# The last RMSNorm of a two-layer diffusion step: weight on ScalarE, factor on VectorE in larger pieces, and the last square in two halves

## The chip, the cores and the metric

The kernel runs on one core of one Trainium2 chip. The metric is the device time of one execution in microseconds (us); several executions are timed and the median is taken. A hardware profile of one further execution gives the trace that the text reads.

## The reference, cut to what matters

Two groups of 128 tokens (a context pass and a denoising step) go through two layers; the model width is 2048. Every layer is a mixer and a gated FFN, each behind an RMSNorm, and a last RMSNorm ends the step:

```
def rmsnorm(x, g):
    xf = x.astype(jnp.float32)
    y = xf * lax.rsqrt(jnp.mean(xf * xf, axis=-1, keepdims=True) + EPS)
    return (y * g.astype(jnp.float32)).astype(x.dtype)
...
        x = x + gt1 * m
        h = rmsnorm(x, g_norm_ffn[l]) * (1 + sc2) + sh2
        x = x + gt2 * conv_ffn(h, w_ffn_up[l], w_ffn_conv[l], b_ffn_conv[l], w_ffn_down[l])
    return rmsnorm(x, g_final), ab_ctx, c_ctx
```

The change concerns the last line, and the sum of squares of the three norms before it and of the last.

## The kernel before, in words

**Layout.** The residual stream `x` lies in SBUF with the features on the 128 partitions, as 16 chunks of 128 features by 256 tokens (128 of each group). A weight matrix comes from HBM in tiles of 1024 KB (SyncE's queue), and every fp32 weight tile is split into a high part `wh` (ScalarE, line 221) and a low part `wl` (VectorE, line 222), in halves of 128x1024, with four buffers of each. TensorE makes three matmuls per 128x128 block (lines 338, 339, 342: `wh` by the high activations, `wh` by the low ones, `wl` by the high ones). At the last chunks before a norm (`QUIET`) the halves are split in two steps of 128x512.

**A chunk's end.** `residual` (line 617) adds a finished chunk to `x` by two VectorE instructions, one for each group of tokens. Where a norm follows, `stat_add` squares the chunk on ScalarE (line 172) and GpSimd adds it to a running sum `sqacc` (line 176); the last chunk's square is not added but kept in `sq`. This is so in the down projections' second half of the inner features (`down`, with `q == NQ - 1`), and in the mixers' output projections.

**The norm.** `stat_rstd` has TensorE sum `sqacc` (line 201) and the last `sq` (line 202) over the partitions, for the one group and then for the other; VectorE scales the result (`rv`, line 184), GpSimd takes the power -1/2 (`rr`, line 188), VectorE makes a diagonal matrix for each group (`diag`, line 208), and TensorE spreads it over the partitions (line 216), so that the factor of every token stands in PSUM on all partitions (`rb`). For the norms inside the layers `modulate` then works out `hx`, chunk by chunk: `nt` (VectorE, line 558; one half scaled by VectorE, line 564, the other by ScalarE, line 567), the high part (ScalarE, line 568), and the low part (VectorE or GpSimd, line 553). `first_three` feeds TensorE with three products at once as the chunks appear (lines 324 to 326), shifted against each other by two chunks.

**The end of the program.** After the last norm's `spread`, 16 VectorE instructions (line 1153) multiply each chunk by the final weight (a value for each partition) and by `rb`; after every four of them a DMA of four chunks, 512 KB, goes to the output (line 1156).

**What sets the order.** Instructions are put in order for each engine when the program is built, by a scheduler that runs the program in a simulated timeline; where the code says so (`keep_in_program_order`, used in `modulate` and `first_three` before layer 1's FFN), the written order holds among the marked instructions. Unmarked ones, such as the splits of weights, are placed around them. So an edit can move instructions elsewhere in the program.

Of the kernel before, what the change touches and what calls it, by code (L numbers as in the profile page):

```python
# [13 lines left out]
AF = mybir.ActivationFunctionType  # L14
ALU = mybir.AluOpType
# [3 lines left out]
P = 128  # L19
D = 2048  # L20
KD = D // P
T = 128
NT = 2 * T
# [10 lines left out]
NQ = 2  # L34
# [51 lines left out]
def step_kernel(ctx: ExitStack, tc: tile.TileContext, A: dict):  # L86
    nc = tc.nc
    pe, dve, act, pool, sp = nc.tensor, nc.vector, nc.scalar, nc.gpsimd, nc.sync
# [20 lines left out]
    def T_(pl, shape, tag, dt=F32, bufs=None):  # L109
        kw = {} if bufs is None else {"bufs": bufs}  # L110
        return pl.tile(shape, dt, tag=tag, name=nm(tag), **kw)
# [8 lines left out]
    def C(name):  # L120
        a, w = _AT[name]
        return cst[:, a:a + w]
# [7 lines left out]
    x = T_(keep, [P, KD, NT], "x")  # L130
# [17 lines left out]
    def step():  # L148
        for g in list(chains):
            if next(g, chains) is chains:  # L150
                chains.remove(g)
# [12 lines left out]
    def stat_add(st, src, n):  # L164

        st["n"] += 1
        if st["n"] == 1:
            st["acc"] = T_(keep, [P, NT], "sqacc")
            act.activation(st["acc"], src, AF.Square)
            return  # L170
        sq = T_(tmp, [P, NT], "sq", bufs=2)
        act.activation(sq, src, AF.Square)  # L172
        if st["n"] == n:
            st["last"] = sq
        else:
            pool.tensor_tensor(out=st["acc"], in0=st["acc"], in1=sq, op=ALU.add)  # L176

    def rstd(cols, n, factor=1.0, out=None):
# [170 lines left out]
    stage = ["ab"]  # L349
# [83 lines left out]
    def feature_step():  # L433

        l, j, q = FEATS[feat["i"]]
        t, c = divmod(feat["t"], 2)
        if c == 0:
            feat["raw"] = T_(wpool, [P, 4, 512], "araw", bufs=2)
            sp.dma_start(out=feat["raw"], in_=A["w_ada"][l, j, q, t])
        feature_sum((l, j, q), t, c, feat["raw"],  # L440
                    T_(feat["pool"], [P, D], "junk").rearrange("p (g n) -> p g n", g=4))
        feat["t"] += 1
        if feat["t"] == 8:
            biased(l, j, q)
            feat["i"] += 1
            feat["t"] = 0
# [10 lines left out]
    def row_step(until=len(ROWS)):  # L457
        if later:
            later.pop(0)()
        if ada["i"] >= until:  # L460
            return
        l, j, q = ROWS[ada["i"]]
        if ada["i"] < 8:
            return pair_step(l, j, q)
        t, g = divmod(ada["t"], 4)
        on_dve = ada["i"] in SUMMED
        if g == 0:
            ada["raw"] = T_(wpool, [P, 4, 512], "araw", bufs=2)
            sp.dma_start(out=ada["raw"], in_=A["w_ada"][l, j, q, t])
        raw = ada["raw"]  # L470
        if on_dve:
            if g % 2:
                feature_sum((l, j, q), t, g // 2, raw, T_(ada["pool"], [P, 4, 512], "junk", BF16, bufs=1))
        elif pinned[0]:
            if g == 1 and t:
                sum_rows(t - 1, ada["last"])
            if g == 3:
                ada["last"] = raw
                if t == 3:
                    last = ada["last"]  # L480
                    later.append(lambda: None)
                    later.append(lambda: sum_rows(3, last))
        elif g == 3:
            sum_rows(t, raw)
        ada["t"] += 1
        if ada["t"] == 16:
            later.extend([lambda: biased(l, j, q)] if on_dve else ada_finish(l, j, q))
            ada["i"] += 1
            ada["t"] = 0
# [25 lines left out]
    def pump(rows, feats=0.0, until=None):  # L515

        until = until or RLIMIT[stage[0]]
        step()
        ada["due"] += rows
        while ada["due"] >= 0.25:  # L520
            if ada["i"] >= until and not later:
                ada["due"] = 0.0
                break
            dve_or_none = ada["i"] >= until or ada["i"] in SUMMED
            ada["due"] -= 0.25 if dve_or_none else 0.25 * ada["pew"]
            row_step(until)
        feat["due"] += feats
        while feat["due"] >= 1.0 and feat["i"] < FLIMIT[stage[0]]:
            feat["due"] -= 1.0
            feature_step()  # L530
# [83 lines left out]
    def residual(ps, l, which, c, st=None):  # L614
        for g in range(2):
            s = slice(g * T, (g + 1) * T)
            dve.scalar_tensor_tensor(out=x[:, c, s], in0=ps[:, s],  # L617
                                     scalar=mod[:, l, 3 * which + 2, c, g:g + 1],
                                     in1=x[:, c, s], op0=ALU.mult, op1=ALU.add)
        if st is not None:  # L620
            stat_add(st, x[:, c], KD)
# [429 lines left out]
    def ffn(hx, W, ready, todo, l, st):  # L1051
        xh, xl = (lambda k: hx[:, k, :NT]), (lambda k: hx[:, k, NT:2 * NT])
        product = lambda: ready.pop(0) if ready else gemm(W.chunk(), xh, xl, between=todo.pop(0) if todo else None)
        WD = Weights(A["w_down"][l], KQ, TB)
        cw = ada["cw"]
        with tc.tile_pool(name=f"ffn{l}", bufs=1) as fp, banks(f"pffn{l}") as pf:
            feat["pool"] = pf
            feat["due"] = 0.0
            T_(fp, [P, SHIFT // 4], "pad")

            def conv(m):
                early = l > 0 and bool(ready)
                pin = tc.keep_in_program_order if early else lambda i: i
                ps = product()
                y = T_(fp, [P, NT], "cv", bufs=3)
                pin(act.activation(y, ps, AF.Identity, scale=cw[:, 1, m:m + 1], bias=cw[:, 3, m:m + 1]))  # L1066
                y3 = y.rearrange("p (g t) -> p g t", g=2)
                p3 = ps.rearrange("p (g t) -> p g t", g=2)
                pin(dve.scalar_tensor_tensor(out=y3[:, :, 1:], in0=p3[:, :, :T - 1],  # L1069
                                             scalar=cw[:, 0, m:m + 1], in1=y3[:, :, 1:],  # L1070
                                             op0=ALU.mult, op1=ALU.add))
                pin(dve.scalar_tensor_tensor(out=y3[:, :, :T - 1], in0=p3[:, :, 1:],  # L1072
                                             scalar=cw[:, 2, m:m + 1], in1=y3[:, :, :T - 1],
                                             op0=ALU.mult, op1=ALU.add))
                if early:
                    W.ahead(pin)
                return y

            def up(q):
                gs = []  # L1080
                for i in range(q * KQ, (q + 1) * KQ):
                    rate = 0 if i < LATE else FRATE["up"]
                    fine[0] = False
                    gate = conv(i)
                    pump(0, rate)
                    val = conv(NFF + i)
                    pump(0, rate)
                    act.activation(gate, gate, AF.Silu)
                    dve.tensor_tensor(out=val, in0=gate, in1=val, op=ALU.mult)
                    g = T_(fp, [P, ROW], "g", F32R, bufs=KQ)  # L1090
                    split(g[:, :NT], g[:, NT:2 * NT], val)
                    gs.append(g)
                    if l == 0 and i == LATE - 1:
                        load_row()
                return gs

            def down(gs, q):
                for c in range(KD):
                    quiet = q == NQ - 1 and c >= KD - QUIET[0]
                    fine[0] = quiet  # L1100
                    ps = gemm(WD.chunk(), lambda k: gs[k][:, :NT], lambda k: gs[k][:, NT:2 * NT])
                    residual(ps, l, 1, c, st if q == NQ - 1 else None)
                    pump(0, 0 if quiet else FRATE["down"])

            for q in range(NQ):
                gs = up(q)
                if q == 0:
                    ensure(l, 5)
                down(gs, q)
            while feat["i"] < FLIMIT[stage[0]]:  # L1110
                feature_step()


    with banks("pab") as ppool["ada"]:
# [5 lines left out]
        for c in range(KD):  # L1120
            sq = T_(tmp, [P, NT], "sq", bufs=2)
# [27 lines left out]
    st = stat_init()  # L1149
    ffn(hx, W, ready, todo, 1, st)  # L1150
    rb = norm_scale(st)
    for c in range(KD):
        dve.scalar_tensor_tensor(out=x[:, c], in0=x[:, c], scalar=C("gfin")[:, c:c + 1], in1=rb,  # L1153
                                 op0=ALU.mult, op1=ALU.mult)
        if c % 4 == 3:
            sp.dma_start(out=A["o_y"][:, c - 3:c + 1], in_=x[:, c - 3:c + 1])

# [132 lines left out]
```

## Time and profile before

| what | value |
|---|---|
| time, three runs | 2353.25 us median (2352.32 to 2356.36) |
| the profiled execution's own time | 2353.05 us |
| its span in the trace | 2351.3 us, so 1.75 us lie around it |
| TensorE matmul | 2304.8 us busy, 98% of the span |
| VectorE, ScalarE, GpSimd | 1780.2, 1163.3, 144.8 us busy |
| the end of the span, from the last product on | about 15 us, without large matmuls |

A row of a timeline has the start and the length in us, then engine, line, operation, output <- inputs, shape, and in brackets how long the engine sat idle ahead of it and what released it. A row with x2 is two like instructions from the start of the first to the end of the last. A line's number is that of the kernel before; in the changed kernel the same statements stand two lines lower from line 178 on, and four lower at the end.

### The profile page before, as it was taken

How to read it: one execution, taken by the hardware profiler on the slowest of the kernel's cores; microseconds unless marked ns; L12 is line 12 of the kernel's file. 1: busy time of each engine (PE TensorE's matmuls, PEld its weight loads, DVE VectorE, ACT ScalarE, POOL GpSimd, SP SyncE). 2: the span in 40 equal slices, each digit the busy share in tenths (PEclk: the TensorE clock that was granted, in tenths of full speed). 3: DMA queues.
4: the chain of work that ended last, by engine and by line, in shares of the span. 5: the costliest groups of instructions: out<-in, count | busy, mean ns of one | idle time of the engine just before them, and what ended most of it. 6: DMA issues, size and time to landing. Idle time of an engine off the chain costs nothing. (4 is left out here: it accounts for less than half of the span.)

```text
span 2351.3 us, 47128 instructions
## 1 busy us (share of the span) xinstructions
PE 2304.8 (98%) x19654; PEld 2190.2 (93%) x19654; DVE 1780.2 (76%) x2662; ACT 1163.3 (49%) x1835; POOL 144.8 (6%) x133
## 2 busy tenths in 40 slices
PE   7999999999999999999999999999999999999997
PEld 6788878799999999999989999898999999999997
DVE  3667554579999999999968889887899755666654
ACT  4346553465554355554455555446555434555542
POOL 0002001100000000001220000022000000000011
PEclk9999999999999999999999999999999999999998
DMA  9887778777777877777767788786677555555553
GB/s 383 338 324 261 256 277 315 306 290 267 267 269 272 309 263 257 264 262 271 293 235 256 262 310 298 300 316 243 221 265 269 198 194 190 192 196 198 196 188 118
DMA packets 92421, 610.81 MB, mean 260 GB/s; under 512 B 9968, under 2 KB 17840, under 8 KB 20528
## 3 DMA queue, kind: packets, MB, share of 16 engines
q1 hardware_dynamic: 92208, 607.80, 70.2%
q8 instruction: 154, 2.52, 0.4%
q14 instruction: 59, 0.48, 0.1%
HBM read 603.01 MB, written 4.75 MB: 258 GB/s over the span
## 5 line engine op out<-in xcount | busy, mean ns | idle before, releaser
L221 ACT CAST wh<-raw 128x1024 fp32r<-128x1024 f32 (+1 forms) x788 | 793.4, 1013 | 947.5 <-PE acc L339 765.1
L222 DVE TENSOR_TENSOR wl<-raw,wh 128x1024 fp32r<-128x1024 f32 (+1 forms) x788 | 922.6, 1186 | 345.2 <-ACT wh L221 326.2
L338 PE MATMUL acc<-hx,wh 128*128 128x256 f32 x3808 | 1058.9, 279 | 5.6 <-ACT hx L568 4.6
L339 PE MATMUL acc<-hx,wh 128*128 128x256 f32 x3808 | 1056.4, 278 | 0.6 <-DVE hx L553 0.6
L342 PE MATMUL acc<-hx,wl 128*128 128x256 f32 x3808 | 1056.5, 278 | 0.0
L338 PEld LDWEIGHTS acc<-hx,wh 128*128 128x128 f32 x3808 | 715.8, 188 | 32.4 <-issue 10.9
L342 PEld LDWEIGHTS acc<-hx,wl 128*128 128x128 f32 x3808 | 716.1, 188 | 10.3 <-issue 9.2
L339 PEld LDWEIGHTS acc<-hx,wh 128*128 128x128 f32 x3808 | 716.8, 188 | 6.3 <-issue 5.0
L429 DVE CUSTOM_DVE_ANT_0 junk<-araw,condb 128x2048 f32<-128x2048 f32 (+1 forms) x176 | 404.0, 2295 | 0.0
L339 PE MATMUL acc<-g,wh 128*128 128x256 f32 x1408 | 388.3, 276 | 0.0
L342 PE MATMUL acc<-g,wl 128*128 128x256 f32 x1408 | 388.0, 276 | 0.0
L338 PE MATMUL acc<-g,wh 128*128 128x256 f32 x1408 | 387.8, 276 | 0.0
L339 PEld LDWEIGHTS acc<-g,wh 128*128 128x128 f32 x1408 | 264.3, 188 | 0.0
L342 PEld LDWEIGHTS acc<-g,wl 128*128 128x128 f32 x1408 | 264.1, 188 | 0.0
L338 PEld LDWEIGHTS acc<-g,wh 128*128 128x128 f32 x1408 | 264.0, 188 | 0.0
L176 POOL TENSOR_TENSOR sqacc<-sqacc,sq 128x256 f32<-128x256 f32 x62 | 83.4, 1344 | 1579.5 <-issue 1291.6
L1066 ACT ACTIVATE cv<-acc,convw 128x256 f32<-128x256 f32 x176 | 98.4, 559 | 3.6 <-PE acc L342 2.0
L617 DVE SCALAR_TENSOR_TENSOR x<-acc,mod,x 128x128 f32<-128x128 f32 x192 | 58.1, 344 | 54.7 <-PE acc L342 54.1
L1069 DVE SCALAR_TENSOR_TENSOR cv<-acc,convw,cv 128x254 f32<-128x254 f32 x176 | 83.8, 476 | 4.6 <-ACT cv L1066 4.6
L1072 DVE SCALAR_TENSOR_TENSOR cv<-acc,convw,cv 128x254 f32<-128x254 f32 x176 | 84.4, 480 | 3.7
L452 PE MATMUL ada<-araw,condw 128*32 128x512 f32 x576 | 79.3, 616 | 4.5 <-DMA araw<-w_ada 4.5
L303 PE MATMUL acc<-wh,hx 128*128 128x256 f32 x256 | 70.3, 281 | 0.9 <-ACT dv L977 0.9
(238 smaller groups left out, 2125.6 us busy)
## 6 DMA issues: line engine op xcount, KB each, us to landing
araw<-w_ada SPq DMA_DIRECT2D x178, 1024.0 KB, 5.5
raw<-w_up SPq DMA_DIRECT2D x176, 1024.0 KB, 4.8
raw<-w_down SPq DMA_DIRECT2D x88, 1024.0 KB, 4.8
raw<-w_in_c SPq DMA_DIRECT2D x48, 1024.0 KB, 6.0
raw<-w_in_ab SPq DMA_DIRECT2D x19, 1024.0 KB, 7.2
raw<-w_out_ab SPq DMA_DIRECT2D x16, 1024.0 KB, 6.9
raw<-w_out_c SPq DMA_DIRECT2D x16, 1024.0 KB, 6.1
condb<-w_ada SPq DMA_DIRECT2D x12, 1024.0 KB, 7.1
```

The lines of the kernel that those rows point to most:

```text
L176: pool.tensor_tensor(out=st["acc"], in0=st["acc"], in1=sq, op=ALU.add)
L221: pin(act.copy(out_hi, src))
L222: pin(dve.tensor_tensor(out=out_lo, in0=src, in1=out_hi.bitcast(F32), op=ALU.subtract))
L303: pe.matmul(ps, hi, wh[:, s], start=a, stop=False)
L338: fixed(pe.matmul(ps[:, :n], wh, xh(k), start=(i == 0), stop=False))
L339: fixed(pe.matmul(ps[:, :n], wh, xl(k), start=False, stop=False))
L342: fixed(pe.matmul(ps[:, :n], wl, xh(k), start=False, stop=(i == last)))
L429: tc.keep_in_program_order(dve.tensor_tensor_reduce(out=junk, in0=raw, in1=condb[:, c].rearrange("p (g n) -> p g n", g=4), scale=1.0, scal ...
L452: i = pe.matmul(ada["ps"][32 * g:32 * g + 32, :], condw[:, 4 * t + g, :], raw[:, g], start=(t == 0), stop=(t == 3), skip_group_check=True)
L1066: pin(act.activation(y, ps, AF.Identity, scale=cw[:, 1, m:m + 1], bias=cw[:, 3, m:m + 1]))
L1069: pin(dve.scalar_tensor_tensor(out=y3[:, :, 1:], in0=p3[:, :, :T - 1], scalar=cw[:, 0, m:m + 1], in1=y3[:, :, 1:], op0=ALU.mult, op1=ALU.add))
L1072: pin(dve.scalar_tensor_tensor(out=y3[:, :, :T - 1], in0=p3[:, :, 1:], scalar=cw[:, 2, m:m + 1], in1=y3[:, :, :T - 1], op0=ALU.mult, op1=A ...
```

## The change

It has three parts. The final weight is applied by ScalarE inside the last `down`, in place, behind each chunk's square. After the last norm only the factor `rb` is left to apply, by five VectorE `tensor_tensor` instructions over 2, 4, 4, 4 and 2 chunks, each with a DMA of its own to the output. And the last chunk's square is made as two halves (one for each group of tokens) at the norms behind stage "ab": before layer 1's mixer, before layer 1's FFN, and the last.

```
         sq = T_(tmp, [P, NT], "sq", bufs=2)
-        act.activation(sq, src, AF.Square)
         if st["n"] == n:
+            for s in ([slice(0, NT)] if stage[0] == "ab" else [slice(0, T), slice(T, NT)]):
+                act.activation(sq[:, s], src[:, s], AF.Square)
             st["last"] = sq
         else:
+            act.activation(sq, src, AF.Square)
             pool.tensor_tensor(out=st["acc"], in0=st["acc"], in1=sq, op=ALU.add)
...
                     residual(ps, l, 1, c, st if q == NQ - 1 else None)
+                    if l == 1 and q == NQ - 1:
+                        act.activation(x[:, c], x[:, c], AF.Identity, scale=C("gfin")[:, c:c + 1])
                     pump(0, 0 if quiet else FRATE["down"])
...
     rb = norm_scale(st)
-    for c in range(KD):
-        dve.scalar_tensor_tensor(out=x[:, c], in0=x[:, c], scalar=C("gfin")[:, c:c + 1], in1=rb,
-                                 op0=ALU.mult, op1=ALU.mult)
-        if c % 4 == 3:
-            sp.dma_start(out=A["o_y"][:, c - 3:c + 1], in_=x[:, c - 3:c + 1])
+    for c, n in ((0, 2), (2, 4), (6, 4), (10, 4), (14, 2)):
+        dve.tensor_tensor(out=x[:, c:c + n], in0=x[:, c:c + n], op=ALU.mult,
+                          in1=rb[:, None, :].to_broadcast([P, n, NT]))
+        sp.dma_start(out=A["o_y"][:, c:c + n], in_=x[:, c:c + n])
```

TensorE's and GpSimd's rows stand in the same order in both programs. Three places show how rows move on the others.

ScalarE at the end of the program, from chunk 14's weights on, before (`wh` is a weight's high part, `sq` a square):

```order
L221 CAST wh_27566<-raw_27564 128x512 x2
L221 CAST wh_27572<-raw_27564 128x512 x2
L172 ACTIVATE sq_27561<-x_76 128x256
L221 CAST wh_27652<-raw_27650 128x512 x2
L221 CAST wh_27658<-raw_27650 128x512 x2
L172 ACTIVATE sq_27647<-x_76 128x256
L172 ACTIVATE sq_27733<-x_76 128x256
```

and of the change, with a row that scales `x` in place (line 1106) behind each square:

```order
L223 CAST wh_27582<-raw_27580 128x512 x2
L223 CAST wh_27588<-raw_27580 128x512 x2
L177 ACTIVATE sq_27576<-x_76 128x256
L223 CAST wh_27669<-raw_27667 128x512 x2
L1106 ACTIVATE x_76<-x_76,cst_74 128x256
L223 CAST wh_27675<-raw_27667 128x512 x2
L177 ACTIVATE sq_27663<-x_76 128x256
L1106 ACTIVATE x_76<-x_76,cst_74 128x256
L174 ACTIVATE sq_27750<-x_76 128x128 x2
L1106 ACTIVATE x_76<-x_76,cst_74 128x256
```

A scaling row comes behind each of the 16 squares, once with two casts between, and the last square is two rows.

VectorE from the last residual to the end, before (`misc` is the factor in PSUM):

```order
L617 SCALAR_TENSOR_TENSOR x_76<-acc_27664,mod_77,x_76 128x128 x2
L184 TENSOR_SCALAR rv_27742<-misc_27737 128x2
L208 TENSOR_SCALAR diag_27746<-cst_74,rr_27744 128x128 x2
L1153 SCALAR_TENSOR_TENSOR x_76<-x_76,cst_74,misc_27749 128x256 x16
L1279 UNCONDITIONAL_BRANCH
```

and of the change:

```order
L619 SCALAR_TENSOR_TENSOR x_76<-acc_27681,mod_77,x_76 128x128 x2
L186 TENSOR_SCALAR rv_27761<-misc_27756 128x2
L210 TENSOR_SCALAR diag_27765<-cst_74,rr_27763 128x128 x2
L1157 TENSOR_TENSOR x_76<-x_76,misc_27768 128x512
L1157 TENSOR_TENSOR x_76<-x_76,misc_27768 128x1024 x3
L1157 TENSOR_TENSOR x_76<-x_76,misc_27768 128x512
```

Sixteen rows have become five; each of the five is followed by its DMA on SyncE's queue.

ScalarE before layer 1's FFN, where `modulate` makes chunks 10 to 14 (`nt`, then the high part in `hx`) while weights are split for `first_three`; before:

```order
L221 CAST wh_19260<-raw_19158 128x1024
L567 ACTIVATE nt_19119<-nt_19119,mod_77,scl_78 128x128
L568 CAST hx_19032<-nt_19119 128x256
L567 ACTIVATE nt_19125<-nt_19125,mod_77,scl_78 128x128
L221 CAST wh_19279<-raw_19160 128x1024
L568 CAST hx_19032<-nt_19125 128x256
L567 ACTIVATE nt_19131<-nt_19131,mod_77,scl_78 128x128
L568 CAST hx_19032<-nt_19131 128x256
L567 ACTIVATE nt_19137<-nt_19137,mod_77,scl_78 128x128
L221 CAST wh_19339<-raw_19337 128x1024
L568 CAST hx_19032<-nt_19137 128x256
L567 ACTIVATE nt_19143<-nt_19143,mod_77,scl_78 128x128
```

and of the change:

```order
L569 ACTIVATE nt_19121<-nt_19121,mod_77,scl_78 128x128
L570 CAST hx_19034<-nt_19121 128x256
L569 ACTIVATE nt_19127<-nt_19127,mod_77,scl_78 128x128
L570 CAST hx_19034<-nt_19127 128x256
L569 ACTIVATE nt_19133<-nt_19133,mod_77,scl_78 128x128
L223 CAST wh_19262<-raw_19160 128x1024
L570 CAST hx_19034<-nt_19133 128x256
L569 ACTIVATE nt_19139<-nt_19139,mod_77,scl_78 128x128
L223 CAST wh_19281<-raw_19162 128x1024
L570 CAST hx_19034<-nt_19139 128x256
L569 ACTIVATE nt_19145<-nt_19145,mod_77,scl_78 128x128
L223 CAST wh_19341<-raw_19339 128x1024
```

The diff says nothing of this place: the scheduler has put the three casts behind more of the chunks' rows (the first of them five rows later), and VectorE's three subtractions that use them have moved back likewise.

## The prediction

> **What bounds the kernel now.** The page's first part comes first: TensorE is busy nearly all the time, so an edit off TensorE's path counts only where TensorE waits.
>
> ```profile
> PE 2304.8 (98%) x19654; PEld 2190.2 (93%) x19654; DVE 1780.2 (76%) x2662; ACT 1163.3 (49%) x1835; POOL 144.8 (6%) x133
> ```
>
> It waits at the norms, and behind the last product it has nothing left. The timeline of the end shows that stretch as one chain in which each row starts when the one ahead of it has ended.
>
> ```profile
> 2336.47 0.61 DVE L617 SCALAR_TENSOR_TENSOR x<-acc,mod,x 128x128 f32<-128x128 f32 x2 [6.87 <-PE acc L342]
> 2337.18 0.42 ACT L172 ACTIVATE sq<-x 128x256 f32<-128x256 f32 x1 [7.06 <-DVE x L617]
> 2337.64 0.38 PE L202 MATMUL misc<-cst,sq 128*128 128x1 f32 x2 [1.09 <-ACT sq L172]
> 2337.89 0.36 PE L201 MATMUL misc<-cst,sqacc 128*128 128x1 f32 x2
> 2338.11 0.36 PE L202 MATMUL misc<-cst,sq 128*128 128x1 f32 x2
> 2338.51 0.16 DVE L184 TENSOR_SCALAR rv<-misc 128x2 f32<-128x2 f32 x1 [1.43 <-PE misc L202]
> 2338.75 0.70 POOL L188 TENSOR_TENSOR rr<-rv,cst 128x2 f32<-128x2 f32 x1 [7.76 <-DVE rv L184]
> 2339.49 0.48 DVE L208 TENSOR_SCALAR diag<-cst,rr 128x128 f32<-128x128 f32 x2 [0.82 <-POOL rr L188]
> 2340.12 1.19 PE L216 MATMUL misc<-diag,cst 128*128 128x256 f32 x2 [1.64 <-DVE diag L208]
> 2341.35 6.36 DVE L1153 SCALAR_TENSOR_TENSOR x<-x,cst,misc 128x256 f32<-128x256 f32 x16 [1.38 <-PE misc L216]
> 2343.03 5.03 SPq L1156 DMA_DIRECT2D o_y<-x  x4
> ```
>
> From 2336.47 to the span's end at 2351.3 are 14.8 us, and the 16 multiplications take 6.36 of them. The last store is issued at about 2347.7 (end of line 1153), and the DMA view tells how long it takes to land.
>
> ```profile
> GB/s 0 0 0 0 0 0 0 0 0 0 0 0 0 0 0 0 0 0 0 0 0 0 0 0 0 335 417 201 395 410 209 410 417 179 417 410 15 0 0 0
> o_y<-x SPq DMA_DIRECT2D x4, 512.0 KB, 2.6
> ```
>
> The slices cover 2330 to 2352, 0.55 us each. Data start in slice 25, about 2343.86, 0.83 behind the first issue; 512 KB at 410 GB/s take 1.28; the rest of the 2.6, about 0.5, lies behind the data. The slices near 200 are gaps: the stores wait for VectorE, not the reverse.
>
> **1. The factor in five pieces.** These groups give the prices of the old and the new instruction.
>
> ```profile
> L1153 DVE SCALAR_TENSOR_TENSOR x<-x,cst,misc 128x256 f32<-128x256 f32 x16 | 6.4, 477 | 1.4 <-PE misc L216 1.4
> L222 DVE TENSOR_TENSOR wl<-raw,wh 128x1024 fp32r<-128x1024 f32 x713 | 872.6, 1236 | 318.2 <-ACT wh L221 301.8 <-PE acc L342 5.0 <-PE acc L326 2.8
> L222 DVE TENSOR_TENSOR oall<-att,oall 128x512 fp32r<-128x512 f32 x8 | 5.5, 686 | 2.4 <-ACT oall L221 2.3
> 1638.03 2.36 DVE L222 TENSOR_TENSOR wl<-raw,wh 128x1024 fp32r<-128x1024 f32 x2
> 2320.74 1.29 DVE L222 TENSOR_TENSOR wl<-raw,wh 128x512 fp32r<-128x512 f32 x2 [1.43 <-ACT wh L221]
> ```
>
> The old one advances by 6.36/16 = 0.40 us per chunk. A `tensor_tensor` takes 1.24 for 1024 elements and 0.69 for 512, the latter with an operand in PSUM (`att`); back to back, a second one starts 2.36 - 1.23 = 1.13 and 1.29 - 0.69 = 0.60 behind the first. So the five end at 0.69, 1.83, 2.96, 4.09 and 0.60 + 3 x 1.13 + 0.69 = 4.68 us, 1.68 sooner than 6.36. No row has a repeated (broadcast) operand from PSUM at this size: the price lies between this and the old 0.40 per chunk, and I take the former, since the 686 ns row has both an operand in PSUM and the pieces' length.
>
> The stores do not follow at that pace. Issued at 0.70, 1.85, 2.98, 4.11 and 4.70, they could start data 0.83 later, but 512 KB need 1.28 and VectorE now delivers them every 1.13: data run 1.53-2.17, 2.68-3.96, 3.96-5.24, 5.24-6.52 and 6.52-7.16. The last lands 0.5 later, at 7.66, against 6.36 + 2.6 = 8.96: **-1.3 us**. What is late next is the store. Bounds: the last store not held up by the fourth lands at 4.70 + 0.83 + 0.64 + 0.5 = 6.67 (-2.3); stores one strictly behind another would end at 9.16 (+0.2). The shorter last store's price is itself between these rows:
>
> ```profile
> o_ckv<-proj SPq DMA_DIRECT2D x1, 256.0 KB, 2.7
> o_gqa_v<-vg SPq DMA_DIRECT2D x1, 128.0 KB, 1.8
> ```
>
> My 0.83 + 0.64 + 0.5 = 2.0 is nearer to the lower; the 2.7 was taken among weight loads.
>
> **2. The last square by halves.** At the end the square waits for both residual instructions. The first half now waits for the first alone, which ends 0.34 after 2336.47. It starts 0.1 later, as now, at 2336.9; its length is 0.42 less 128 elements. The slope comes from
>
> ```profile
> L568 ACT CAST hx<-nt 128x256 fp32r<-128x256 f32 x64 | 24.4, 403 | 7.3 <-DVE nt L564 5.8 <-DVE nt L558 0.8
> L221 ACT CAST wh<-raw 128x1024 fp32r<-128x1024 f32 x713 | 749.8, 1054 | 893.1 <-PE acc L339 727.1 <-issue 66.4 <-ACT g L221 48.7
> ```
>
> (1054 - 403)/768 = 0.85 ns per element, so 0.31 us. TensorE's first line 202 moves from 2337.64 to 2337.25: **-0.39**. The second half ends about 2337.49; TensorE asks for it 0.47 behind the first (2338.11 - 2337.64), at 2337.72, so it is not late.
>
> At the two inner norms ScalarE's queue sets the start; this is the one at 1605, the other (1189) has the same lengths.
>
> ```profile
> 1604.76 1.04 ACT L221 CAST wh<-raw 128x1024 fp32r<-128x1024 f32 x1 [1.68 <-PE acc L339]
> 1605.71 0.41 ACT L172 ACTIVATE sq<-x 128x256 f32<-128x256 f32 x1
> 1606.17 0.38 PE L202 MATMUL att<-cst,sq 128*128 128x1 f32 x2 [1.28 <-ACT sq L172]
> ```
>
> There the residuals were long done; only the shorter first half counts, 0.1 each: **-0.2**. An instruction more on ScalarE costs 0.1 at its end, and nobody waits for that.
>
> **3. Sixteen scalings on ScalarE.** Price and cover:
>
> ```profile
> L719 ACT ACTIVATE nt<-proj,cst 128x256 f32<-128x256 f32 x6 | 3.0, 498 | 0.0
> 2317.36 1.14 ACT L221 CAST wh<-raw 128x512 fp32r<-128x512 f32 x2 [1.25 <-issue]
> 2270.00:2300.00 30.00, 30.00 (x267) 30.00 (x266) 15.73 (x20) 13.01 (x16) 4.97 (x4) 1.00 0.57 205
> ```
>
> The like instruction takes 0.50 us, 8.0 in all. Each also waits for its square's end, with a weight split queued behind. In the 30 us window ScalarE (the fourth engine) is busy 13.0 and TensorE never idles. A buffer of 8 blocks feeds TensorE for 8 x 3 x 0.113 = 2.7 us, and with three other buffers ahead of it a split made at 2317.36 and subtracted by 2319.3 is wanted about 6 us later. A delay of 0.6 is hidden: **0**. Without that cover it would be +8.0. The last scaling ends near 2338.1, long before the piece that needs it.
>
> [...]
>
> **4. The moved casts before layer 1's FFN.** `first_three` needs the second chunk's second half of weights (the first cast of the three) at 1623.2, its low part at 1623.39.
>
> ```profile
> 1610.27 0.49 ACT L567 ACTIVATE nt<-nt,mod,scl 128x128 f32<-128x128 f32 x1 [4.14 <-DVE nt L558]
> 1610.79 0.41 ACT L568 CAST hx<-nt 128x256 fp32r<-128x256 f32 x1
> 1611.10 0.49 ACT L567 ACTIVATE nt<-nt,mod,scl 128x128 f32<-128x128 f32 x1
> 1619.73 1.05 ACT L221 CAST wh<-raw 128x1024 fp32r<-128x1024 f32 x1
> 1621.69 1.22 DVE L222 TENSOR_TENSOR wl<-raw,wh 128x1024 fp32r<-128x1024 f32 x1
> 1623.39 0.28 PE L326 MATMUL acc<-hx,wl 128*128 128x256 f32 x1
> 1628.00 0.28 PE L324 MATMUL acc<-hx,wh 128*128 128x256 f32 x1
> 1629.07 0.39 PE L325 MATMUL acc<-hx,wh 128*128 128x256 f32 x1 [0.79 <-POOL hx L553]
> 1630.10 0.28 PE L324 MATMUL acc<-hx,wh 128*128 128x256 f32 x1
> 1630.46 0.38 PE L325 MATMUL acc<-hx,wh 128*128 128x256 f32 x1
> ```
>
> Now the low part is ready at 1622.91, 0.5 early. Five rows later on ScalarE are some 2.2 us (two casts and three scalings at the first rows' steps of 0.31 and 0.52); the cast then ends near 1623.1 and the low part near 1624.4: a stall of 1.0. In exchange the late chunks come 1 to 2 us sooner, and TensorE's later waits for chunks 14 and 15 go: 1629.07 - 1628.00 and 1630.46 - 1630.10, less a step of 0.11 each, are 0.96 + 0.25 = 1.2. Bounds +1.0 and -1.2; both happen by this account, so I take **-0.2**.
>
> **Sum:** -1.3 - 0.39 - 0.2 - 0.2 = -2.1 on the profiled execution's 2353.05, which is 0.2 below the median of the runs: **2351.0 us**.
>
> **Rivals.** *Stores freer.* The last store isn't held up (-2.3) and part 4 gains all (-1.2); with part 2's 0.6 that is -4.1, 2349.0. For it: 417 GB/s is the most that one store at a time shows, and two together are never seen. Against: adjacent slices agree at 410 to 417. *Stores one behind another.* Nothing here shows two stores overlap; then +0.2 - 0.8 = -0.6, 2352.5. [...] *The pieces are no faster.* The broadcast operand keeps the old pace, and only the shorter last store gains 0.6: with parts 2 and 4 -1.4, 2351.6. *ScalarE becomes the path.* If splits come late by their scaling, which needs a lead below 0.6 us in the last down projection instead of 6, the 16 x 0.5 = 8.0 stand in TensorE's rows: 8.0 - 2.1 = +5.9, 2359.0, slower than before.
>
> **How the numbers follow.** Forecast 0.62, freer stores 0.15, stores in series 0.12, no faster pieces 0.06, ScalarE 0.05. A measurement of this kernel tells about 0.2% (4.7 us) from no change. Faster by that: half of the freer stores and the forecast's edge by the runs' spread, 0.10; slower: the last rival, 0.05; within: 0.85. The range 2348.8 to 2354.2 goes from the freer stores to the stores in series (2352.5) with part 4 at +1.0 in place of -0.2 and 0.5 for the runs' spread; it leaves out the last rival and the edges.
>
> **What would show it.** Line 1157's rows ending 4.7 us behind their start (6.3: third rival); GB/s near 410 without gaps behind the second store (gaps: stores in series); line 204's first row 0.8 us behind the first residual at the end instead of 1.17; no TensorE wait in the last down projection; line 326 waiting about 1 us near 1624 and no waits near 1629. A last store landing later than 8 us behind the first piece's start would make the forecast wrong.

## The result, and the profile after

Before: 2353.82 us median of 22 runs (2352.32 to 2356.72). The change: 2351.19 us median of 22 runs (2347.69 to 2354.54). The ratio is 0.9988, with a 95% interval from 0.9983 to 0.9994: 1.4 to 4.0 us faster, 2.6 by the medians. 2351.0 was forecast, 2.1 below the profiled execution of before. The change is measurable, and smaller than the 0.2% bound (4.7 us).

The change's profiled execution has a span of 2348.4 us against 2351.3. Not all of the 2.9 us are the change's: two executions already differ by some us where the first changed row stands (last section). So what follows compares stretches: the time between two rows of one trace.

The end of the changed kernel, its timeline from the last residual on:

```profile
2335.33 0.61 DVE L619 SCALAR_TENSOR_TENSOR x<-acc,mod,x 128x128 f32<-128x128 f32 x2 [6.87 <-PE acc L344]
2335.78 0.51 ACT L174 ACTIVATE sq<-x 128x128 f32<-128x128 f32 x2 [6.26 <-DVE x L619]
2336.14 0.38 PE L204 MATMUL misc<-cst,sq 128*128 128x1 f32 x2 [0.73 <-ACT sq L174]
2336.32 0.51 ACT L1106 ACTIVATE x<-x,cst 128x256 f32<-128x256 f32 x1
2336.61 0.36 PE L204 MATMUL misc<-cst,sq 128*128 128x1 f32 x2
2338.61 1.16 PE L218 MATMUL misc<-diag,cst 128*128 128x256 f32 x2 [1.64 <-DVE diag L210]
2339.81 4.68 DVE L1157 TENSOR_TENSOR x<-x,misc 128x512 f32<-128x512 f32 x5 [1.34 <-PE misc L218]
2340.52 4.32 SPq L1159 DMA_DIRECT2D o_y<-x  x5
```

From the first row to the span's end are 2348.4 - 2335.33 = 13.07 us, against 2351.3 - 2336.47 = 14.83: 1.76 less. The first half of the square is now what TensorE waits for, and TensorE starts on it 0.81 us behind the start of the residual instead of 1.17. The five pieces take 4.68 us instead of 6.36; from the first piece to the span's end the gain is 1.36 us. The spread took 1.16 us instead of 1.19.

The stores of the changed kernel, in a DMA view of 2327 to 2349 (slices of 0.55 us; the last number of a row is the median from issue to landing):

```profile
GB/s 0 0 0 0 0 0 0 0 0 0 0 0 0 0 0 0 0 0 0 0 0 0 0 0 0 0 324 153 350 402 417 395 395 417 417 350 194 0 0 0
o_y<-x SPq DMA_DIRECT2D x3, 512.0 KB, 2.8
o_y<-x SPq DMA_DIRECT2D x2, 256.0 KB, 2.5
```

and the landings of all five in the view of `o_y`:

```profile
DMA to landing us min/median/max: 2.0/2.8/3.0
```

Before, the row fell to about 200 between stores. Now there is one gap, behind the small first store, and then no slice below 350 until the last. The first 256 KB land in 2.0 us, the last in 3.0: the last store is 1.0 late because data ahead of it are still moving.

Before layer 1's FFN, TensorE's rows near the moved casts:

```profile
1621.97 0.28 PE L328 MATMUL acc<-hx,wl 128*128 128x256 f32 x1
1622.38 0.39 PE L326 MATMUL acc<-hx,wh 128*128 128x256 f32 x1
1622.60 0.28 PE L327 MATMUL acc<-hx,wh 128*128 128x256 f32 x1
1623.64 0.38 PE L328 MATMUL acc<-hx,wl 128*128 128x256 f32 x1 [0.76 <-DVE wl L224]
```

The wait for the low part is there (1623.64 - 1622.60 less a step of 0.11, 0.93 us), and so is one for the cast itself ahead of 1622.38 (0.30). In return the late waits are gone. The product that stood at 1629.07 before, 0.96 us late, is the second of these rows of the change:

```profile
1628.06 0.28 PE L326 MATMUL acc<-hx,wh 128*128 128x256 f32 x1
1628.17 0.28 PE L327 MATMUL acc<-hx,wh 128*128 128x256 f32 x1
```

Behind 1623.86 no step up to the first product made one chunk at a time is longer than 0.16 us. What remains of the two is read from the first row of `modulate` to the first product made one chunk at a time; before:

```profile
1609.81 0.42 DVE L558 TENSOR_TENSOR nt<-x,att 128x256 f32<-128x256 f32 x1 [1.31 <-PE att L216]
...
1632.85 0.28 PE L338 MATMUL acc<-hx,wh 128*128 128x256 f32 x1
```

and of the change:

```profile
1608.74 0.42 DVE L560 TENSOR_TENSOR nt<-x,att 128x256 f32<-128x256 f32 x1 [0.98 <-PE att L218]
...
1631.59 0.28 PE L340 MATMUL acc<-hx,wh 128*128 128x256 f32 x1
```

23.04 us have become 22.85: 0.19 less.

At the inner norm ahead of it, the last of TensorE's sums and `rv`, VectorE's row that takes them up; before:

```profile
1606.64 0.36 PE L202 MATMUL att<-cst,sq 128*128 128x1 f32 x2
1607.04 0.16 DVE L184 TENSOR_SCALAR rv<-att 128x2 f32<-128x2 f32 x1
```

and of the change, with the weight split that VectorE makes ahead of `rv`:

```profile
1605.17 1.23 DVE L224 TENSOR_TENSOR wl<-raw,wh 128x1024 fp32r<-128x1024 f32 x1 [0.41 <-ACT wh L223]
1605.87 0.36 PE L204 MATMUL att<-cst,sq 128*128 128x1 f32 x2
1606.31 0.15 DVE L186 TENSOR_SCALAR rv<-att 128x2 f32<-128x2 f32 x1
```

The sums come sooner, but VectorE's split ends only at 1605.17 + 1.23 = 1606.40, and `rv` starts 0.44 us behind the last sum's start instead of 0.40. From the square's start (1605.71 before, 1605.04 in the change) to `rv` are 1.27 us instead of 1.33: 0.06 of the 0.1 us arrive.

### The profile page after: what moved, and what is told of

It is laid out like the page before. It is cut to its first block, busy times and chain, and to the rows that moved or that the text cites. A ratio compares the mean times of both kernels' runs of the same rounds, so it can differ in the third digit from the quotient of the medians.

```text
span 2348.4 us, 47120 instructions
## 1 busy us (share of the span) xinstructions
PE 2303.5 (98%) x19654; PEld 2189.2 (93%) x19654; DVE 1777.2 (76%) x2651; ACT 1171.6 (50%) x1854; POOL 144.9 (6%) x133
## 4 chain that ended last, share of the span: by engine, by line
PE 94%; DVE 2%; DMA 1%; ACT 1%; issue 1%; POOL 0%; DVEq 0%; POOLq 0%; ACTq 0%
PE acc L340 27%; PE acc L344 27%; PE acc L341 27%; PE ada L454 3%; PE acc L305 1%; PE acc L306 1%; PE acc L308 1%; DMA araw<-w_ada 1%; PE att L667 1%; DVE wl L224 1%; PE acc L327 1%; ACT wh L223 1%; PE acc L328 0%; DVE nt L566 0%; PE acc L326 0%
```

## The experiments

My theory: the gain comes at the end (the pieces, limited by the stores, and the first half of the square) with small sums at the inner norms; the scaling is hidden. The rivals: the scaling costs by its price; the moved casts carry the gain or a loss; the last store is held by its queue or by a fixed time of each store, not by moving data.

A run's ratio is its time over that of the kernel before, timed beside it, with a 95% interval. The kernels by the same stretches, from each one's timeline, in us: from the last chunk's first residual to the first row of line 202 (204), the spread's length, from the first piece to the span's end, `modulate` to the first single product before layer 1's FFN, and from there to the last residual.

| kernel | square ready | spread | pieces and stores | `modulate` to product | layer 1's FFN |
|---|---|---|---|---|---|
| before | 1.17 | 1.19 | 9.95 | 23.04 | 703.62 |
| the change | 0.81 | 1.16 | 8.59 | 22.85 | 703.74 |
| whole_squares | 1.17 | 1.19 | 8.59 | 23.04 | 703.62 |
| halves_alone | 0.80 | 1.19 | 9.91 | 22.93 | 703.75 |
| scaling_alone | 1.17 | 0.67 | 9.93 | 23.03 | 703.62 |
| last_halves | 0.80 | 1.19 | 8.57 | 23.04 | 703.63 |
| sixteen_products | 0.80 | 0.67 | 8.98 | 22.79 | 703.63 |
| two_queues | 0.80 | 1.19 | 8.66 | 22.77 | 703.63 |
| five_scalings | 0.80 | 0.92 | 8.57 | 22.78 | 703.62 |
| six_pieces | 0.81 | 1.19 | 8.64 | 22.77 | 703.62 |
| no_fourth_store | 0.81 | 1.19 | 7.63 | 22.92 | 703.74 |
| filled_wait | 0.81 | 0.67 | 8.57 | 22.93 | 703.75 |

**Without the halves.** `whole_squares`:

```
-            for s in ([slice(0, NT)] if stage[0] == "ab" else [slice(0, T), slice(T, NT)]):
+            for s in [slice(0, NT)]:
```

> The scaling on ScalarE and the five pieces without the halved squares; the casts before layer 1's FFN stand again as before. My theory (the gain is the end, set by the stores): from the first residual of the last chunk to the span's end 13.5 us, that is 14.8 of before less 1.3; line 204's first row 1.17 us behind that residual again; about 2352.5 us. Rival (the gain of the change came from the moved casts or the halves): 14.8 us at the end, no gain.

Measured: 2353.05 us, ratio 0.9997 (0.9988 to 1.0006); the end 2354.6 - 2341.14 = 13.46 us.

```profile
2342.31 0.38 PE L204 MATMUL misc<-cst,sq 128*128 128x1 f32 x2 [1.09 <-ACT sq L174]
2346.01 4.68 DVE L1157 TENSOR_TENSOR x<-x,misc 128x512 f32<-128x512 f32 x5 [1.38 <-PE misc L218]
```

The square is as late as before and the pieces as short as in the change: pieces and stores give 1.36 us by themselves. The median doesn't tell 1.3 us from nothing here; the trace does.

**The halves alone**, `halves_alone`, the change without its other edits:

```
-                    if l == 1 and q == NQ - 1:
-                        act.activation(x[:, c], x[:, c], AF.Identity, scale=C("gfin")[:, c:c + 1])
...
-    for c, n in ((0, 2), (2, 4), (6, 4), (10, 4), (14, 2)):
...
+    for c in range(KD):
+        dve.scalar_tensor_tensor(out=x[:, c], in0=x[:, c], scalar=C("gfin")[:, c:c + 1], in1=rb,
+                                 op0=ALU.mult, op1=ALU.mult)
```

> Only the halved squares, with before's sixteen multiplications and four stores; the casts stand as in the change. My theory: line 204's first row 0.8 us behind the first residual at the end, the end 0.4 shorter (14.4 us), 0.1 at each inner norm, and a wait of about 1.2 us near the moved casts that is given back by the waits of the last chunks: 0.6 to 0.8 faster than before in all, 2353.1. Rival (the moved casts are a loss): the stretch from the square before layer 1's FFN to the first product of one chunk at a time is longer than before's 27.1 us.

Measured: 2353.54 us, ratio 0.9997 (0.9988 to 1.0005). The end is 2349.6 - 2335.19 = 14.41 us, and from the square before layer 1's FFN (1604.48) to the first single product (1631.44) 26.96 us against before's 27.14, of which 0.11 lie behind `modulate`'s first row: the moved casts are no loss.

**The scaling alone**, `scaling_alone`:

```
-            for s in ([slice(0, NT)] if stage[0] == "ab" else [slice(0, T), slice(T, NT)]):
+            for s in [slice(0, NT)]:
...
-    for c, n in ((0, 2), (2, 4), (6, 4), (10, 4), (14, 2)):
...
+    for c in range(KD):
+        dve.scalar_tensor_tensor(out=x[:, c], in0=x[:, c], scalar=ones[:, 0:1], in1=rb,
+                                 op0=ALU.mult, op1=ALU.mult)
```

> The sixteen scalings on ScalarE, and the old sixteen multiplications with a column of ones in place of the weight, so that VectorE and the stores keep their old work. My theory: hidden, no TensorE wait in the last down projection, the end at 14.8 us as before, time as before within 0.5 us. Rival (ScalarE's work by its price): up to 8 us slower, with waits of TensorE for the split weights.

Measured: 2354.75 us, ratio 1.0004 (0.9995 to 1.0012); layer 1's FFN 703.62 us, to the hundredth that of before; the end 14.28 us, 0.5 below the expected 14.8 because the spread took 0.67 us in this execution (see `filled_wait`).

**Five times the scaling**, `five_scalings`:

```
                         act.activation(x[:, c], x[:, c], AF.Identity, scale=C("gfin")[:, c:c + 1])
+                        for _ in range(4):
+                            act.activation(T_(tmp, [P, NT], "nt", bufs=4), x[:, c], AF.Identity, scale=C("gfin")[:, c:c + 1])
```

> The change with four more scalings behind each chunk's, into a buffer that nothing reads: ScalarE has 64 instructions more of about 0.4 us, 26 us in the last down projection. My theory (a lead of about 6 us per weight half against 2.1 us more): no TensorE wait there, the end that of the change, time that of the change within 0.5 us. Rival (no lead): TensorE waits, up to 26 us slower.

Measured: 2352.26 us, ratio 0.9998 (0.9989 to 1.0006); layer 1's FFN 703.62 us. The busy times of 1640 to 2330, in the change and here (engines PE, PEld, DVE, ACT, POOL):

```profile
1640.00:2330.00 690.00, 690.00 (x6090) 690.00 (x6090) 480.55 (x634) 346.19 (x461) 16.16 (x14) 1.00 0.58 206
```

```profile
1640.00:2330.00 690.00, 690.00 (x6089) 689.19 (x6082) 482.83 (x636) 371.39 (x521) 15.50 (x13) 1.00 0.59 209
```

ScalarE worked 25 us more and TensorE was busy throughout.

**Halves at the last norm only**, `last_halves`:

```
-            for s in ([slice(0, NT)] if stage[0] == "ab" else [slice(0, T), slice(T, NT)]):
+            for s in ([slice(0, NT)] if stage[0] != "ffn1" else [slice(0, T), slice(T, NT)]):
```

> The change with whole squares at the two inner norms, so that the casts before layer 1's FFN stand as before. My theory: the end is that of the change (13.1 us), and the stretch before layer 1's FFN is that of before (27.1 us from the square to the first product of one chunk at a time, against 26.6 in the change): 0.5 us slower than the change at most, about 2351.7. Rival (the moved casts carry the gain): as slow as before.

Measured: 2352.44 us, ratio 0.9991 (0.9983 to 1.0); the end 2350.0 - 2336.93 = 13.07 us, that of the change, and 23.04 us from `modulate` to the product, that of before (from the square it is 26.90 instead of the expected 27.1, since the spread of that norm took 0.98 us here and 1.22 before). In the order of instructions the three casts stand as before in the three kernels with whole squares at the inner norms, and moved in all others: it is the inner halves that move them.

**Sixteen products**, `sixteen_products`:

```
-    for c, n in ((0, 2), (2, 4), (6, 4), (10, 4), (14, 2)):
...
+    for c in range(KD):
+        dve.tensor_tensor(out=x[:, c], in0=x[:, c], in1=rb, op=ALU.mult)
+        if c % 4 == 3:
+            sp.dma_start(out=A["o_y"][:, c - 3:c + 1], in_=x[:, c - 3:c + 1])
```

> The change, but the factor by sixteen tensor_tensor products of one chunk and four stores of four chunks. My theory (part of the gain is the kind of instruction, part the size): a product starts 0.33 us behind the one ahead, sixteen end at 5.4 us; the four stores' data run at about 410 GB/s and the last lands near 8.0 us behind the first product's start, against 7.7 in the change and 9.0 before: the end 0.3 longer than the change's. Rival (only the size of the pieces counts): 6.4 us and the end 1.3 longer than the change's.

Measured: 2353.03 us, ratio 0.9995 (0.9986 to 1.0003).

```profile
2342.32 5.39 DVE L1157 TENSOR_TENSOR x<-x,misc 128x256 f32<-128x256 f32 x16 [0.85 <-PE misc L218]
```

5.39 of the 6.36 us: the product without a second factor for each partition starts every 0.33 instead of 0.39 us. Pieces and stores take 8.98, of the change's 1.36 us gain 0.97; the larger pieces and the shorter last store give the remaining 0.39.

**Two queues**, `two_queues`:

```
-        sp.dma_start(out=A["o_y"][:, c:c + n], in_=x[:, c:c + n])
+        (act if c in (2, 10) else sp).dma_start(out=A["o_y"][:, c:c + n], in_=x[:, c:c + n])
```

> The change with the second and the fourth store issued by ScalarE. My theory (the stores share the same 410 GB/s): data without a gap from the second store on, the last lands at about 7.7 us behind the first piece's start as in the change. Rival (the last store is held up by its queue): it lands 2.0 us behind its issue at 4.7, at 6.7, and the end is 1.0 shorter.

Measured: 2351.94 us, ratio 0.9994 (0.9986 to 1.0003); pieces and stores 8.66 us, no gain. Taking the fourth store out of the last one's queue doesn't bring the last data forward.

**Six pieces**, `six_pieces`:

```
-    for c, n in ((0, 2), (2, 4), (6, 4), (10, 4), (14, 2)):
+    for c, n in ((0, 1), (1, 2), (3, 3), (6, 4), (10, 4), (14, 2)):
```

> The change with six pieces of 1, 2, 3, 4, 4 and 2 chunks, so that the first store starts sooner. My theory: the first store is issued 0.45 us behind the first piece's start instead of 0.71, the gaps between the first stores remain, and the last lands 7.6 instead of 7.7 us behind it: 0.1 us shorter. Rival (a store's own fixed time counts each time): one store more, 0.5 us or more longer.

Measured: 2351.42 us, ratio 0.9988 (0.9979 to 0.9997). The first store is issued 2340.41 - 2339.96 = 0.45 us in, as expected, but pieces and stores take 8.64: the expected 0.1 shorter did not come, nor 0.5 longer. What the earlier start gave was lost again behind it: in slices of 0.265 us the stores' rate falls three times (to 174, 135 and 209 GB/s) before it stays at 340 or more until the last, where the change has one gap (0 GB/s in a slice of 0.26 us). Why is not settled.

**No fourth store**, `no_fourth_store`:

```
-        sp.dma_start(out=A["o_y"][:, c:c + n], in_=x[:, c:c + n])
+        if c != 10:
+            sp.dma_start(out=A["o_y"][:, c:c + n], in_=x[:, c:c + n])
```

> The change without the fourth store: chunks 10 to 13 are multiplied but not written to the output. My theory (the last store is late since its data wait for the fourth's): it lands 2.0 us behind its issue instead of 3.0, and from the first piece's start to the span's end are 7.6 us instead of 8.6. Rival (its landing takes 3.0 of itself, or the pieces set the end): 8.6 us again.

Measured: 2351.33 us, ratio 0.9985 (0.9975 to 0.9995). Its stores, in a DMA view, and its pieces, in the timeline:

```profile
o_y<-x SPq DMA_DIRECT2D x2, 256.0 KB, 2.0
```

```profile
2342.67 4.68 DVE L1157 TENSOR_TENSOR x<-x,misc 128x512 f32<-128x512 f32 x5 [1.38 <-PE misc L218]
```

Both stores of 256 KB now land in 2.0 us (that group's median), and from the first piece to the span's end are 2350.3 - 2342.67 = 7.63 us instead of 8.59. The last store's third microsecond was the wait for the fourth store's data.

**Work in TensorE's last wait**, `filled_wait`. The spread had taken 1.2 us in most traces and 0.67 in two; this run asks why.

```
         for g in range(2):
...
+        if stage[0] == "ffn1":
+            idle = T_(pacc, [P, 512], "acc")
+            for _ in range(13):
+                tc.keep_in_program_order(pe.matmul(idle[:, :NT], hx[:, 0, :P], hx[:, 0, :NT], start=True, stop=True))
         return rstd([ps[:, 0:2]], 2, **kw)
```

> The change with 13 matmuls of 128x256 (their product is read by nothing) on TensorE behind line 204's last row, while VectorE and GpSimd work out the diagonal. My theory (the spread takes 1.2 us instead of 0.67 where the granted clock has fallen to half in the wait): the clock stays near 1 up to the spread, which takes 0.67 us, and the end from the last residual on is 12.6 us instead of 13.1. Rival (the length of the spread has another cause, or 1.5 us of matmuls come too late): 1.2 us and 13.1, or longer by the tail of the added matmuls.

Measured: 2351.89 us, ratio 0.9991 (0.9982 to 1.0). Its timeline:

```profile
2338.44 1.79 PE L210 MATMUL acc<-hx 128*128 128x256 f32 x13
2340.22 0.67 PE L224 MATMUL misc<-diag,cst 128*128 128x256 f32 x2
```

and a window ahead of the spread and into it (the number behind POOL's busy time is the granted clock):

```profile
2339.00:2340.50 1.50, 1.50 (x12) 1.32 (x11) 0.48 (x2) 0.00 (x0) 0.56 (x1) 1.00 0.00 0
```

In the kernel before, in a window around the spread:

```profile
2339.67:2341.37 1.70, 1.19 (x2) 0.50 (x2) 0.32 (x3) 0.00 (x0) 0.00 (x0) 0.50 0.00 0
```

The spread took 1.19 us at a clock of 0.50 and 0.67 at 1.00. From the last residual to the span's end are 2349.5 - 2336.94 = 12.56 us, 2.27 less than before and 0.51 less than in the change. The median, 2.8 us below that of before timed beside it, does not tell this kernel from the change. Nor does this one trace prove that the added matmuls held the clock: in `scaling_alone` and `sixteen_products` the spread ran at 1.00 without them. A window of `sixteen_products` around its spread:

```profile
2341.50:2342.40 0.90, 0.67 (x2) 0.30 (x2) 0.08 (x1) 0.00 (x0) 0.00 (x0) 1.00 0.00 0
```

How long the clock stayed at 1.00 in each trace is in the last section.

## Why the prediction was right

**The five pieces: right.** 4.68 us forecast and measured; the repeated operand in PSUM costs nothing that shows, and the third rival falls. Pieces and stores gave 1.36 us (9.95 to 8.59) against 1.3; the last store, issued at 2344.5, lands 3.0 us later, 7.7 behind the first piece's start as forecast. The data of the last store were forecast to wait for the fourth's, and `no_fourth_store` shows that they do. "Freer stores" and "stores one behind another" both fell: in the slices the data of one store follow the other's at once, at about 400 GB/s; behind one early gap the stores of 512 and 256 KB moved their data at 350 to 417 GB/s.

**The halves: right at the end, too large at the inner norms.** The end's first row of line 204 came 0.36 us sooner against 0.39 forecast. At both inner norms TensorE's row comes 0.1 us sooner, as forecast (1605.40 - 1605.04 = 0.36 us from the square to TensorE's row, 1606.17 - 1605.71 = 0.46 before). But the prediction took that 0.1 for the gain and left out VectorE's weight split, shown above for one of them: from the square to the spread are 2.78 us instead of 2.84 at both, so 0.06 are left at each, 0.12 together against 0.2.

**The scaling at nothing: right.** Layer 1's FFN takes 703.62 us without scalings in the kernel before, with sixteen in `scaling_alone` and with eighty in `five_scalings`. One scaling takes 0.51 us on ScalarE, and a chunk's old multiplication on VectorE took 0.40. The higher price did not count, since ScalarE had time to spare: it was busy for 346 of 690 us with sixteen scalings and for 371 with eighty. The last rival fell with it.

**The moved casts: right in the mechanism, in the size partly by luck.** +1.0 and -1.2 were forecast, -0.2 together. In the change 1.23 us of wait appeared (0.93 for the low part, 0.30 for the cast, which the prediction had not counted), and the two late waits of 0.96 and 0.25 went, and with them one of 0.19 (ahead of 1625.36 before) that it had not listed. Two errors of 0.2 cancelled. The stretch is 0.19 us shorter in the change and 0.11 to 0.27 shorter in the others that have the move.

**The sum.** 1.76 at the end, 0.12 at the inner norms and 0.19 at the casts are 2.07 us, 2.1 forecast; the runs' interval, 1.4 to 4.0, holds it. What of the median's 2.6 goes beyond it stays open, since the runs scatter by more. That the time came within 0.2 us of 2351.0 is luck in part: the forecast started from 2353.05, and the median of the 22 runs of before is 2353.82.

## What to carry to other kernels

Where the last stage writes out as fast as it computes, price the stores' data as well as the instructions: a fifth of VectorE's gain (1.68 us of which 1.36 arrived) went behind the store ahead here. Split an instruction when its first half has an earlier input and a consumer of its own, and look in the built order for what the split moves elsewhere. When an effect is smaller than the scatter of the runs, read it between two rows of one trace.

## What the runs showed of the hardware that was not expected

**The clock at the end.** Behind the last product TensorE has only eight 128x1 matmuls until the spread, which starts 3.3 us later (3.7 with whole squares). The spread then took 1.16 to 1.19 us in eight of the eleven traces without added work, 0.92 in one and 0.67 in two. In the traces with a window around the spread the granted clock was 0.50 where it took 1.19 and 1.00 where it took 0.67. For eight of the eleven the time is known at which the clock fell from 1.00 to 0.50: for the first two from windows of 0.25 us, for the others as an estimate from the mean clock of a window of 1.7 or 2.4 us that holds the fall.

| kernel | clock fell, us behind the last product | spread |
|---|---|---|
| before | 2.3 | 1.19 |
| the change | 3.3 | 1.16 |
| whole_squares | 2.8 | 1.19 |
| six_pieces | 2.9 | 1.19 |
| last_halves | 3.1 | 1.19 |
| five_scalings | 3.6 | 0.92 |
| sixteen_products | 4.2 | 0.67 |
| scaling_alone | 4.8 | 0.67 |

No relation to the edits shows. The fall came ahead of the spread (1.19), in it (0.92, and 1.16 in the change) or behind its end (0.67). So half a microsecond of the end hangs on when the clock falls, and that it fell before or early in the spread both in the kernel before and in the change is luck for their comparison. The eight 128x1 matmuls did not hold it: in the kernel before it fell at 2338.7, 0.2 us behind the end of the last of them (2338.47). In `filled_wait` it was 1.00 up to 2340.50, 3.6 us behind the last product, with the spread (from 2340.22) under way. Two traces without added work kept it longer (4.2 and 4.8), so that 13 matmuls of 128x256 hold it is not shown.

**Where the runs scatter.** Until the square before layer 1's FFN, executions differ by up to 6 us (1604.48 in `halves_alone`, 1610.47 in `whole_squares`), with no relation to the edits that shows; from the first single product of layer 1's FFN to the last residual they take 703.62 to 703.75 us. Most of the scatter is made early: TensorE's first row on the last chunk's square stands at 452.6 to 458.1 us in ten of the traces at the norm before layer 0's FFN, and at 1187.3 to 1193.2 before layer 1's mixer, the first place that the change touches. TensorE's waits for the weights `araw` from HBM in the first 1600 us differ as well (4.5 us in the kernel before, 5.5 in the change), but not in step with the times: the change reaches the norm before layer 1's mixer 2.0 us sooner (1187.33 against 1189.32). What makes the scatter was not tried.
